# A hybrid trunk on one core: the output projection of the first three tiles moved between the steps of the attention

## The chip, the cores and the metric

The kernel runs on 1 core of a Trainium2 chip. The metric is the device time of one execution in microseconds, the median of three runs.

## What is computed

Two layers, each a pre-norm, one input projection, four branches with a gate each, one output projection, a post-norm and a residual. The sequence has 1024 positions and the model width is 1024; the branches are 256 wide each. The change touches the last two lines of the loop and the attention, cut here to what matters:

```python
def mla_branch(cq, ckv, k_rope, gate, positions, qa_g, qb_w, kva_g, kvb_w):
    q = (rms_norm(cq, qa_g) @ qb_w).reshape(bsz, s, D_HEADS, D_NOPE + D_ROPE)
    ...
    def attend(inp):
        qb, qch = inp
        sc = jnp.einsum('bqhd,bkhd->bhqk', qb, k).astype(jnp.float32) * scale
        mask = key_chunk[None, :] <= qch[:, None]
        p = jax.nn.softmax(jnp.where(mask, sc, MASK_VALUE), axis=-1).astype(v.dtype)
        return jnp.einsum('bhqk,bkhd->bqhd', p, v)
    ...
    return o * jax.nn.silu(gate)

def reference(...):
    for l in range(DEPTH):
        h = rms_norm(x, pre_norm_g[l])
        proj = h @ w_in[l]
        ...
        y = jnp.concatenate([y_a, y_b, y_c, y_d], axis=-1) @ w_out[l]
        x = x + rms_norm(y, post_norm_g[l])
    return x
```

`y_a` is a convolution branch, `y_b` a gated linear recurrence, `y_c` a chunked state-space scan, `y_d` the attention above, causal by blocks. So a query tile late in the sequence has long scores, one early in it has short ones.

## The kernel before

**Tiles.** The sequence is cut into 8 token tiles of 128 rows. From the attention on they are taken from the last to the first: `ORDER` is 7, 6, ..., 0. Products with weights are made in three passes, high part by high part, high by low and low by high (`wh`, `wl` are the two parts of a weight, `yh`, `yl` of the activations).

**Order of work.** Each stage is a Python generator, a "thread"; `weave` takes the next step from the thread whose planned position is lowest (`PLAN` gives start, end and count of steps). A scheduler afterwards orders the instructions of each engine; each engine then works its own list in order. DMAs are issued from SP, POOL and ScalarE.

**Attention**, `th_att`, per tile two half-steps `m` of two heads each: scores `psc` on TensorE (a large PSUM buffer, of which there are two), their maximum `nm` on VectorE (L912), the exponentials `pe` on ScalarE (L914, 7 buffers of the `k4` kind), then transposes `ptp` (L923), copies `pT`, and the product with the values into `poD` (L927). Between them `q_steps` (L861) makes the queries of a later tile: product `pq`, scaling `qk` on ScalarE, rotation on VectorE, transposes `ptq`. At a tile's end the reciprocal of the sums is spread over 256 columns on VectorE (`rsD`, L934), transposed (`prsD`, L937), multiplied with the gate (`gD`) and the result `yD` is stored by POOL into a buffer in memory, `yspF` (L942). Short PSUM tiles come from two small pools of two buffers each, `smA` (`ptp`, `prsD`, `pty` among others) and `smB` (`poD`, `pq`, `ptq`).

**Output projection.** `th_w` loads `w_out` in 8 chunks and splits them. `out_a` (L963) loads one tile of the concatenated branches by two SP transfers, casts and subtracts one half of it (`yh`, `yl`), transposes the other half (`pty`) and does the same. `out_b` (L977) makes the 48 products of a tile (`pz`, L991). `th_o` (L996) does `out_a`, `out_b` of tile 7 and `out_a` of tile 6 at the end of the attention.

**Last phase of a layer.** For each tile `out_b` of it, `out_a` of the one two later, and `out_c` (L1032): load of the residual tile `xt` (2 buffers), Square with its sum on ScalarE into the scratch tile `hn` (2 buffers, L1043), product with the post-norm row `gpost` on VectorE into `zt` (L1044), reciprocal root by two short ScalarE steps (L142, L143), residual (L1049), store; in layer 0 also the next layer's pre-norm: Square (L233), `hn` (L235), 8 transposes `pst` (L239), their split `hh`, `hl`. In layer 1 the result goes out. `th_v` of the next layer (projection rows `psV`) is the first work that uses `hh`, tile by tile.

## Time and profile before

| | us |
|---|---|
| median of three runs | 1264.37 (1259.96 to 1267.64) |
| the profiled execution | 1263.69 |
| its span in the trace | 1261.9 |
| TensorE busy in it | 1197.7 (95%) |
| VectorE busy | 836.2 (66%) |
| ScalarE busy | 478.5 (38%) |
| POOL busy | 183.1 (15%) |

The busy times come from one execution. Matmul ends are modelled in it and overlap the next start, so the busy share of TensorE is not the share in which it does useful work at its full rate; where exact lengths matter they are taken from start to start. Two places matter for what follows: the attention of layer 0 ends at 541 us and that of layer 1 at 1161 us, and the products of layer 0's last phase end at 640 us. A row of a timeline gives in brackets the idle time of its engine ahead of it and what ended that.

### The profile page before, as it was taken

How to read it: one execution, taken by the hardware profiler on the slowest of the kernel's cores; microseconds unless marked ns; L12 is line 12 of the kernel's file. 1: busy time of each engine (PE TensorE's matmuls, PEld its weight loads, DVE VectorE, ACT ScalarE, POOL GpSimd, SP SyncE). 2: the span in 40 equal slices, each digit the busy share in tenths (PEclk: the TensorE clock that was granted, in tenths of full speed). 3: DMA queues.
4: the chain of work that ended last, by engine and by line, in shares of the span. 5: the costliest groups of instructions: out<-in, count | busy, mean ns of one | idle time of the engine just before them, and what ended most of it. 6: DMA issues, size and time to landing. Idle time of an engine off the chain costs nothing.

```text
span 1261.9 us, 17853 instructions
## 1 busy us (share of the span) xinstructions
PE 1197.7 (95%) x6902; PEld 987.0 (78%) x6902; DVE 836.2 (66%) x1579; ACT 478.5 (38%) x1088; POOL 183.1 (15%) x290
## 2 busy tenths in 40 slices
PE   5999999899989989999999999998999998999997
PEld 5988899888878746678898889897888776566886
DVE  5566999985376386745454859999754763867232
ACT  5413322233474374433432222321435644644211
POOL 2100011201133111210020001211012322112000
PEclk9999999999999989989999999998999899999999
DMA  7001122201151040244221111211114311202531
GB/s 274 34 34 68 44 83 85 76 34 48 62 156 61 22 153 23 66 148 147 101 97 67 34 51 59 92 52 67 35 61 123 106 36 54 93 18 68 188 129 71
DMA packets 38660, 101.47 MB, mean 80 GB/s; under 512 B 5440, under 2 KB 13808, under 8 KB 38576
## 3 DMA queue, kind: packets, MB, share of 16 engines
q1 hardware_dynamic: 22848, 51.42, 11.9%
q0 software_dynamic: 14864, 46.04, 11.1%
q10 hardware_dynamic: 864, 2.88, 0.6%
q8 instruction: 54, 0.88, 0.3%
q14 instruction: 30, 0.25, 0.1%
HBM read 75.37 MB, written 25.20 MB: 80 GB/s over the span
## 4 chain that ended last, share of the span: by engine, by line
PE 76%; DVE 14%; ACT 3%; DMA 3%; issue 2%; POOL 0%; DVEq 0%; POOLq 0%; ACTq 0%
PE pz L991 13%; PE psx L220 4%; PE psx L223 4%; PE psx L226 4%; PE psc L909 3%; DVE ca L481 3%; PE plB L625 2%; PE psA L220 2%; PE psA L223 2%; PE psA L226 2%; PE poD L927 2%; PE ptp L923 2%; PE psgA L347 2%; PE psgA L348 2%; PE psgA L349 2%
## 5 line engine op out<-in xcount | busy, mean ns | idle before, releaser
L481 DVE SCALAR_TENSOR_TENSOR ca<-hpad,col,ca 128x512 f32<-128x512 f32 x240 | 186.3, 782 | 3.9
L176 DVE TENSOR_TENSOR wl<-raw,wh 128x1024 fp32r<-128x1024 f32 (+2 forms) x56 | 66.9, 1195 | 92.0 <-ACT wh L160 91.9
L160 ACT CAST wh<-raw 128x1024 fp32r<-128x1024 f32 (+2 forms) x56 | 57.5, 1027 | 139.8 <-PE psA L223 33.7
L991 PE MATMUL pz<-woh,yh 128*128 128x512 f32 x240 | 78.2, 405 | 0.2 <-ACT yh L160 0.2
L991 PE MATMUL pz<-woh,yl 128*128 128x512 f32 x240 | 75.7, 397 | 0.0
L991 PE MATMUL pz<-wol,yh 128*128 128x512 f32 x240 | 75.7, 397 | 0.0
L209 PE MATMUL psg<-wh,hh 128*128 128x256 f32 x256 | 73.9, 289 | 1.5 <-ACT gt L160 1.4
L909 PE MATMUL psc<-kT,qTt 96*128 96x512 f32 (+4 forms) x192 | 73.2, 505 | 0.9 <-ACT pe L914 0.8
L210 PE MATMUL psg<-wl,hh 128*128 128x256 f32 x256 | 73.2, 286 | 0.0
L211 PE MATMUL psg<-wh,hl 128*128 128x256 f32 x256 | 72.8, 284 | 0.0
L914 ACT ACTIVATE pe<-psc,nm 128x1024 f32<-128x1024 f32 (+7 forms) x64 | 47.2, 739 | 64.3 <-DVE nm L912 63.8
L625 PE MATMUL plB<-qz,krb 128*128 128x128 f32 x448 | 63.0, 288 | 8.5 <-DVE krb L635 8.5
L625 PEld LDWEIGHTS plB<-qz,krb 128*128 128x128 f32 x448 | 58.3, 200 | 10.7 <-issue 5.5
L220 PE MATMUL psx<-hh,wh 128*128 128x512 f32 x192 | 62.3, 403 | 0.0
L719 DVE SCALAR_TENSOR_TENSOR xbc<-xpad,col,xbc 128x512 f32<-128x512 f32 x72 | 51.1, 748 | 16.3 <-ACT xbc L172 15.5
L223 PE MATMUL psx<-hl,wh 128*128 128x512 f32 x192 | 61.7, 401 | 0.0
L226 PE MATMUL psx<-hh,wl 128*128 128x512 f32 x192 | 61.1, 397 | 0.0
L991 PEld LDWEIGHTS pz<-wol,yh 128*128 128x128 f32 x240 | 45.6, 190 | 10.6
L176 DVE TENSOR_TENSOR yl<-yt,yh 128x512 fp32r<-128x512 f32 x16 | 11.0, 690 | 64.7 <-ACT yh L160 64.7
L912 DVE TENSOR_REDUCE nm<-psc 128x1 f32<-128x1024 f32 (+7 forms) x64 | 47.2, 745 | 9.9 <-PE psc L909 9.9
L991 PEld LDWEIGHTS pz<-woh,yl 128*128 128x128 f32 x240 | 45.3, 189 | 10.6 <-issue 0.2
L991 PEld LDWEIGHTS pz<-woh,yh 128*128 128x128 f32 x240 | 44.9, 190 | 9.8 <-ACT yh L160 0.4
(331 smaller groups left out, 3052.3 us busy)
## 6 DMA issues: line engine op xcount, KB each, us to landing
raw<-in_w_dram SPq DMA_DIRECT2D x44, 512.0 KB, 3.4
rawo<-in_wo_dram SPq DMA_DIRECT2D x16, 512.0 KB, 4.1
gsp<-gt POOLq DMA_DIRECT2D x16, 256.0 KB, 2.5
gl<-gsp POOLq DMA_DIRECT2D x8, 512.0 KB, 5.0
gspF<-gtA POOLq DMA_DIRECT2D x16, 256.0 KB, 2.3
ysp<-gl POOLq DMA_DIRECT2D x8, 512.0 KB, 3.4
lm<-acsp POOLq DMA_DIRECT2D x16, 256.0 KB, 4.0
yt<-ysp SPq DMA_DIRECT2D x16, 256.0 KB, 3.4
```

What stands on the lines that cost most here:

```text
L160: (V.tensor_copy if name in ONV else A.copy)(out_, in_)
L176: V.tensor_tensor(lo, src, hi.bitcast(F32), op=ALU.subtract)
L209: T.matmul(ps[:, :n], a, hs[k], start=(k == 0), stop=False)
L210: T.matmul(ps[:, :n], a, ls[k], start=False, stop=False)
L211: T.matmul(ps[:, :n], b, hs[k], start=False, stop=(k == KD - 1))
L220: T.matmul(ps[:, h * 512:(h + 1) * 512], w, hh[:, k, h * 512:(h + 1) * 512], start=(k == 0), stop=False)
L223: T.matmul(ps[:, h * 512:(h + 1) * 512], w, hl[:, k, h * 512:(h + 1) * 512], start=False, stop=False)
L226: T.matmul(ps[:, h * 512:(h + 1) * 512], wl, hh[:, k, h * 512:(h + 1) * 512], start=False, stop=(k == KD - 1))
L481: V.scalar_tensor_tensor(t, hp[:, k:k + 512], w[k], t, op0=ALU.mult, op1=ALU.add)
L625: T.matmul(pl[:, o0:o0 + P].rearrange("p (r b u) -> p r b u", r=2, u=u), k_[:, t_ * P:(t_ + 1) * P], z[:, :, t_ * P:(t_ + 1) * P].rearrang ...
L909: T.matmul(psc[:, c0:c1_], qTt[0:k_, h, :], kT[h, c0 // 512][0:k_, 0:c1_ - c0], start=True, stop=True)
L991: T.matmul(pz[n], a[:, k, :], w[:, k, n * 512:(n + 1) * 512], start=(k == 0 and a is yh and w is wh), stop=(k == KD - 1 and a is yl))
```

## The change

Attention and output projection are woven into each other. `th_o` is no longer a thread of the plan but is stepped from `th_att`: at the end of the second tile its first step (a load of `gpost` by POOL and `out_a` of tile 7), then one quarter, 12 products of 512 columns (`pzh`, in a small `smB` bank), after the scores of each half-step of the tiles from the third on. Two quarters make half the columns of an output tile, four a tile, so 12 quarters make the tiles 7, 6 and 5. After each half `post` makes its Square sum and its product with `gpost`; the products are kept in `zt` tiles that take buffers of the weight pools `raw` (twice) and `wh`. Then `out_b` of tile 4 and `out_a` of tile 3 follow. The last phase makes the remaining tiles, and behind the `out_c` of each of the first three of them also the `out_c` of one of the kept tiles. The transposes `prsD` lie in the second half of the bank of `poD`, and the reciprocal is taken on 4 columns, with a copy that spreads it. `w_out` is planned earlier (`w0`, `w1`). The first projection of layer 1 takes the tiles in the order `RORDER`, the order in which the last phase finishes them.

```diff
@@ -23,6 +23,8 @@
+OUT0, NOUT = 2, 3
...
...
+RORDER = [ORDER[n] for n in (3, 0, 4, 1, 5, 2, 6, 7)]
...
-    "o0": (482.2, 511, 8.2),
...
-    "w0": (452.3, 481.6, 8),
+    "w0": (374, 398, 8),
...
@@ -79,9 +82,8 @@
     "c1": (275.5, 340.6, 48.2),
     "d1": (266.1, 351.4, 72),
     "q1": (335.5, 349.5, 2),
-    "o1": (479.4, 508.2, 8.2),
     "att1": (347.1, 481.6, 144.8),
-    "w1": (452.7, 453.2, 8),
+    "w1": (352, 385, 8),
 }
 
 
...
@@ -385,7 +387,7 @@
             hs, ls = load_chunk(l, "v")
             nc.gpsimd.dma_start(out=row, in_=rows[l].partition_broadcast(P))
             nc.gpsimd.dma_start(out=col, in_=cols[l])
-            for n_, i in enumerate(ORDER if l > 0 else range(NT)):
+            for n_, i in enumerate(RORDER if l > 0 else range(NT)):
                 if l == 0:
                     load_x(i + 3)
                     if i > 0:
...
@@ -820,7 +822,7 @@
                 proj_tok(hT, hs, ls, i, ND, ps)
                 ms = small(2, "msd", 3)
                 cn = tmp(384, "cn")
-                jd = br.tile([P, 384], BF16, tag="jd", name="jd", bufs=1)
+                jd = br.tile([P, 384], BF16, tag="jd", name="jd", bufs=1, padded_shape=[P, 512])
                 copy("cn", cn, ps[:, 0:384])
                 krd = small(32, "krd", 2, (P, 2, 16))
                 copy("krd", krd.rearrange("p a j -> p (a j)"), ps[:, 384:416])
...
@@ -890,11 +892,13 @@
             yield next(q_steps)
 
         def th_att():
-            for i in ORDER:
+            outs = th_o()
+            for n_, i in enumerate(ORDER):
                 qTt = qTs[i]
                 n = (i + 1) * P
 
-                po = sm("poD")[:, 0:256]
+                pob = sm("poD")
+                po, prs = pob[:, 0:256], pob[:, 256:512]
                 sume = small(4, "sume", 2)
                 gt = tmp(256, "gD", (P, 2, P))
                 nc.gpsimd.dma_start(out=gt, in_=feat(gspF, 1, i * P, (i + 1) * P))
...
@@ -914,6 +918,8 @@
                         A.activation(pe[:, 0:n], psc[:, 0:n], AF.Exp, bias=nm, accum_out=sume[:, h:h + 1])
                         pes.append(pe)
                     yield i + 1
+                    if n_ >= OUT0:
+                        next(outs, None)
                     for j0 in range(0, i + 1, 4):
                         j1 = min(i + 1, j0 + 4)
                         pts = []
...
@@ -931,8 +937,8 @@
                         next(q_steps, None)
                     yield i + 1
                 rs = tmp(256, "rsD", (P, 4, 64))
-                V.reciprocal(rs, sume.unsqueeze(2).to_broadcast([P, 4, 64]))
-                prs = sm("prsD")[:, 0:256]
+                V.reciprocal(sume, sume)
+                V.tensor_copy(rs, sume.unsqueeze(2).to_broadcast([P, 4, 64]))
                 for m in range(2):
                     T.transpose(prs[:, m * P:(m + 1) * P], rs[:, 2 * m:2 * m + 2, :].rearrange("p h d -> p (h d)"), idn)
                 gf = gt.rearrange("p m t -> p (m t)")
...
@@ -940,7 +946,10 @@
                 y = tmp(256, "yD")
                 V.tensor_tensor(y, po, gf, op=ALU.mult)
                 nc.gpsimd.dma_start(out=feat(yspF, 1, i * P, (i + 1) * P), in_=y.rearrange("p (m t) -> p m t", m=2))
+                if n_ == OUT0 - 1:
+                    next(outs)
                 yield 0.1
+            yield from outs
 
 
         wo_t = {}
...
@@ -993,11 +1002,40 @@
                     yield 1
             zs[i] = pz if halves else [pzb]
 
+        def post(pz, gpost, hv, zt, hn, ss):
+
+            A.activation(hn, pz, AF.Square, scale=1.0 / 32, accum_out=ss)
+            V.tensor_tensor(zt[:, hv], pz, gpost[:, hv], op=ALU.mult)
+
         def th_o():
+
+            gpost = k4("gpost")
+            nc.gpsimd.dma_start(out=gpost, in_=post_g[l].partition_broadcast(P))
             out_a(ORDER[0], lambda: k4("yt"))
             yield 0.1
-            yield from out_b(ORDER[0])
-            out_a(ORDER[1], lambda: k4("yt"))
+            wh, wl = wo_t["h"], wo_t["l"]
+            for n_, i in enumerate(ORDER[:NOUT]):
+                yh, yl = ys[i]
+                zt = wst.tile([P, D], F32, tag=("raw", "raw", "wh")[n_], padded_shape=[P, 1040], name="zt",
+                              bufs=(NRAW, NRAW, NWH)[n_])
+                ss = lay.tile([P, 2], F32, tag="sso", name="sso", bufs=NOUT)
+                for h in range(2):
+                    hv = slice(h * 512, (h + 1) * 512)
+                    pz = sm("pzh")
+                    for k in range(KD):
+                        for a, w in ((yh, wh), (yh, wl), (yl, wh)):
+                            T.matmul(pz, a[:, k, :], w[:, k, hv], start=(k == 0 and a is yh and w is wh),
+                                     stop=(k == KD - 1 and a is yl))
+                        if k == 3:
+                            yield 1
+                    jd = br.tile([P, 512], BF16, tag="jd", name="jz", bufs=1)
+                    post(pz, gpost, hv, zt, jd, ss[:, h:h + 1])
+                    if h == 1:
+                        out_a(ORDER[n_ + 1], lambda: k4("yt"))
+                    yield 1
+                zs[i] = zt, ss
+            yield from out_b(ORDER[NOUT])
+            out_a(ORDER[NOUT + 1], lambda: k4("yt"))
             yield 0.1
 
         def plan(name):
...
@@ -1015,7 +1053,7 @@
         wpool = tc.alloc_tile_pool(name=f"wo{l}", bufs=1, side=my)
         wo_t["h"] = wpool.tile([P, KD, D], F32R, name=f"woh{l}")
         wo_t["l"] = wpool.tile([P, KD, D], F32R, name=f"wol{l}")
-        ths += [Thread(th_att(), *plan("att")), Thread(th_w(), *plan("w")), Thread(th_o(), *plan("o"))]
+        ths += [Thread(th_att(), *plan("att")), Thread(th_w(), *plan("w"))]
         weave(ths, 1e9)
         br.release()
         if l + 1 < L:
...
@@ -1030,18 +1068,20 @@
             gpre = op.tile([P, D], F32, tag="gpre", name="gpre")
             nc.gpsimd.dma_start(out=gpre, in_=pre_g[l + 1].partition_broadcast(P))
         def out_c(i):
-            pz = zs[i]
             tsl = slice(i * P, (i + 1) * P)
             xt = op.tile([P, D], F32, tag="xt", name="xt", bufs=2)
             nc.gpsimd.dma_start(out=xt, in_=(x if l == 0 else xsp)[tsl, :])
-            zt = op.tile([P, D], F32, tag="zt", name="zt", bufs=1)
             hn = op.tile([P, D], F32, tag="hn", name="hn", bufs=2)
-            ss = op.tile([P, 2], F32, tag="ss", name="ssz", bufs=4)
-            nh = len(pz)
-            hv = [slice(h * (D // nh), (h + 1) * (D // nh)) for h in range(nh)]
-            for h, c in enumerate(hv):
-                A.activation(hn[:, c], pz[h], AF.Square, scale=1.0 / 32, accum_out=ss[:, h:h + 1])
-                V.tensor_tensor(zt[:, c], pz[h], gpost[:, c], op=ALU.mult)
+            if isinstance(zs[i], tuple):
+                zt, ss = zs[i]
+                nh, hv = 2, [slice(0, D)]
+            else:
+                zt = op.tile([P, D], F32, tag="zt", name="zt", bufs=1)
+                ss = op.tile([P, 2], F32, tag="ss", name="ssz", bufs=4)
+                nh = len(zs[i])
+                hv = [slice(h * (D // nh), (h + 1) * (D // nh)) for h in range(nh)]
+                for h, c in enumerate(hv):
+                    post(zs[i][h], gpost, c, zt, hn[:, c], ss[:, h:h + 1])
             if nh == 2:
                 V.tensor_tensor(ss[:, 0:1], ss[:, 0:1], ss[:, 1:2], op=ALU.add)
             rstd(ss[:, 0:1], ss[:, 0:1])
...
@@ -1053,13 +1093,16 @@
                 nc.gpsimd.dma_start(out=xsp[tsl, :], in_=xt)
                 pre_norm(hn, xt, gpre, hTn, i)
 
-        for n, i in enumerate(ORDER):
-            if n > 0:
-                for _ in out_b(i):
+
+        for m in range(NOUT, NT):
+            if m + 1 < NT:
+                for _ in out_b(ORDER[m + 1]):
                     pass
-            if n + 2 < NT:
-                out_a(ORDER[n + 2], lambda: op.tile([P, D], F32, tag="yt", name="yt", bufs=2))
-            out_c(i)
+            if m + 2 < NT:
+                out_a(ORDER[m + 2], lambda: op.tile([P, D], F32, tag="yt", name="yt", bufs=2))
+            out_c(ORDER[m])
+            if m - NOUT < NOUT:
+                out_c(ORDER[m - NOUT])
         op.release()
         wpool.release()
         hT = hTn
```

TensorE, layer 0, end of the attention. Names: `ptp` transposes of exponentials, `psc` scores, `prsD` transposes of the reciprocal, `poD` product with the values, `pty` transposes of the branch output, `pz` output products. Before:

```order
L923 MATMUL ptp<-idn,pe 128x128
L909 MATMUL psc<-kT,qTt 128x128
L923 MATMUL ptp<-idn,pe 128x128
L909 MATMUL psc<-kT,qTt 128x128
L937 MATMUL prsD<-idn,rsD 128x128 x2
L923 MATMUL ptp<-idn,pe 128x128
L927 MATMUL poD<-pT,vD 64x128 x2
L923 MATMUL ptp<-idn,pe 128x128
L973 MATMUL pty<-idn,yt 128x128 x4
L937 MATMUL prsD<-idn,rsD 128x128 x2
L927 MATMUL poD<-pT,vD 64x128 x2
L973 MATMUL pty<-idn,yt 128x128 x4
```

After (the quarters are `pzh`, and the reciprocal's transposes are written into `poD`):

```order
L1027 MATMUL pzh<-wol_3926,yh 128x512
L929 MATMUL ptp<-idn,pe 128x128
L913 MATMUL psc<-kT,qTt 128x128
L1027 MATMUL pzh<-woh_3925,yl 128x512
L1027 MATMUL pzh<-woh_3925,yh 128x512
L1027 MATMUL pzh<-wol_3926,yh 128x512
L1027 MATMUL pzh<-woh_3925,yl 128x512
L933 MATMUL poD<-pT,vD 64x128 x2
L982 MATMUL pty<-idn,yt 128x128 x4
L929 MATMUL ptp<-idn,pe 128x128 x2
L1000 MATMUL pz<-woh_3925,yh 128x512 x2
L1000 MATMUL pz<-wol_3926,yh 128x512 x2
```

The rows of tile 0's attention stood next to each other; now products of an output tile lie between them.

ScalarE, layer 0, the attention from tile 6 to tile 5. Names: `pe` exponentials, `qk` scaled queries, `qTt` their transposes copied, `pT` copied transposes of exponentials, `yh` the cast branch output. Before:

```order
L914 ACTIVATE pe,sume<-psc,nm 128x896
L914 ACTIVATE pe,sume<-psc,nm 128x768 x3
L166 ACTIVATE qk<-pq,rq 128x384
L914 ACTIVATE pe,sume<-psc,nm 128x768
L160 COPY qTt<-ptq 96x512
L160 COPY pT<-ptp 128x384
```

After:

```order
L918 ACTIVATE pe,sume<-psc,nm 128x896
L918 ACTIVATE pe,sume<-psc,nm 128x768 x3
L162 CAST yh<-yt 128x4x128
L168 ACTIVATE qk<-pq,rq 128x384
L918 ACTIVATE pe,sume<-psc,nm 128x768
L162 COPY qTt<-ptq 96x512
L162 COPY pT<-ptp 128x384
L162 CAST yh<-pty 128x4x128
```

The two casts of tile 7's branch output now stand in the attention, the first of them ahead of `qk`.

ScalarE, at the end of layer 0's last phase. Names: `hh` cast transposes of the pre-norm, `hn<-xt` Square of the pre-norm, `hn<-pz` Square of the post-norm, `ss`, `ssz` reciprocal roots, `wh<-raw` a weight of layer 1. Before:

```order
L160 CAST hh_4898<-pst 128x4x128 x2
L233 ACTIVATE hn,ss<-xt 128x1024
L142 ACTIVATE ss<-ss,eps 128x1
L143 ACTIVATE ss<-ss 128x1
L160 CAST wh<-raw 128x1024
L1043 ACTIVATE hn,ssz<-pz 128x1024
L160 CAST hh_4898<-pst 128x4x128 x2
L142 ACTIVATE ssz<-ssz,eps 128x1
L143 ACTIVATE ssz<-ssz 128x1
L233 ACTIVATE hn,ss<-xt 128x1024
```

After:

```order
L162 CAST hh_5116<-pst 128x4x128 x2
L1007 ACTIVATE hn,ssz<-pz 128x1024
L144 ACTIVATE ssz<-ssz,eps 128x1
L145 ACTIVATE ssz<-ssz 128x1
L162 CAST wh<-raw 128x1024
L235 ACTIVATE hn,ss<-xt 128x1024
L162 CAST hh_5116<-pst 128x4x128 x2
L1007 ACTIVATE hn,ssz<-pz 128x1024
L144 ACTIVATE ss<-ss,eps 128x1
L144 ACTIVATE ssz<-ssz,eps 128x1
L145 ACTIVATE ss<-ss 128x1
L145 ACTIVATE ssz<-ssz 128x1
```

Two finishing steps are in hand at once there: the short steps of both stand in pairs, and the last post-norm Square stands behind the second pair of casts `hh`.

## Rows read from the trace of the kernel before

**Rows 1.** The page, part 4: chain that ended last, share of the span by engine.

```profile
PE 76%; DVE 14%; ACT 3%; DMA 3%; issue 2%; POOL 0%; DVEq 0%; POOLq 0%; ACTq 0%
```

**Rows 2.** The chain, 536 to 570 us; columns: start us, us, what.

```profile
541.18 12.90 PE pz L991 x48
554.08 0.44 PE pty L973 x4
554.52 11.13 PE pz L991 x48
```

**Rows 3.** Groups of TensorE, 526.9 to 540.8 us; columns: busy, mean, idle before, releasers.

```profile
L923 PE MATMUL ptp<-idn,pe 128*128 128x128 f32 x12 | 2.9, 296 | 1.1 <-ACT pe L914 1.1
L909 PE MATMUL psc<-kT,qTt 100*128 100x128 f32 (+1 forms) x12 | 2.5, 309 | 0.0
L927 PE MATMUL poD<-pT,vD 128*64 128x128 f32 x26 | 2.5, 308 | 0.1
L973 PE MATMUL pty<-idn,yt 128*128 128x128 f32 x8 | 1.7, 354 | 0.0
L937 PE MATMUL prsD<-idn,rsD 128*128 128x128 f32 x6 | 1.6, 350 | 1.9 <-DVE rsD L934 1.7 <-ACT qTt L160 0.2
L866 PE MATMUL pq<-qbt,cqT 128*128 128x384 f32 x4 | 1.6, 512 | 0.0
L879 PE MATMUL ptq<-idn,qk 128*96 128x128 f32 x4 | 0.6, 272 | 0.0
```

**Rows 4.** TensorE's timeline, 503 to 512 us; columns: start us, us, what, count.

```profile
506.53 1.09 PE L927 MATMUL poD<-pT,vD 128*64 128x128 f32 x16
507.55 1.56 PE L866 MATMUL pq<-qbt,cqT 128*128 128x384 f32 x4
508.95 1.02 PE L909 MATMUL psc<-kT,qTt 100*128 100x512 f32 x2
```

**Rows 5.** Mean by stretch; columns: us, busy by engine, TensorE clock, DMA, GB/s.

```profile
538.10:544.90 6.80, 6.08 (x20) 4.55 (x21) 3.96 (x8) 1.71 (x4) 1.44 (x2) 0.50 0.12 39
859.00:863.00 4.00, 0.65 (x6) 0.46 (x5) 4.00 (x7) 0.75 (x2) 0.71 (x1) 0.92 0.16 66
862.40:872.60 10.20, 8.08 (x29) 7.09 (x30) 10.20 (x19) 1.45 (x4) 0.00 (x0) 0.50 0.30 104
1151.00:1161.50 10.50, 8.81 (x60) 5.85 (x60) 8.15 (x23) 5.94 (x21) 2.12 (x3) 1.00 0.37 116
```

**Rows 6.** Timeline, layer 0, 497 to 503 us; in brackets idle before and releaser.

```profile
500.49 1.09 PE L927 MATMUL poD<-pT,vD 128*64 128x128 f32 x16 [0.56 <-DVE pT L160]
```

**Rows 7.** Timeline, layer 1, 1086 to 1094 us.

```profile
1092.37 1.77 PE L909 MATMUL psc<-kT,qTt 96*128 96x512 f32 x4 [0.80 <-ACT pe L914]
```

**Rows 8.** Timeline, layer 0, 475 to 485 us.

```profile
477.80 0.73 POOL L942 DMA_DIRECT2D yspF<-yD  x1 [2.21 <-DVE yD L941]
...
483.37 0.58 ACT L166 ACTIVATE qk<-pq,rq 128x384 f32<-128x384 f32 x1 [0.43 <-PE pq L866]
```

**Rows 9.** DMA issues; columns: queue, count, KB each, median us to landing.

```profile
yt<-yspF SPq DMA_DIRECT2D x16, 256.0 KB, 3.9
xt<-in_x_dram POOLq DMA_DIRECT2D x8, 512.0 KB, 4.2
xsp<-xt POOLq DMA_DIRECT2D x8, 512.0 KB, 2.9
...
yspF<-yD POOLq DMA_DIRECT2D x16, 128.0 KB, 2.2
gpost<-in_post_g_dram POOLq DMA_DIRECT2D x2, 512.0 KB, 6.7
```

**Rows 10.** Timeline, from layer 0 to layer 1, 639 to 652 us.

```profile
640.35 1.02 ACT L1043 ACTIVATE hn<-pz 128x1024 f32<-128x1024 f32 x1
...
643.96 1.28 DVE L1049 SCALAR_TENSOR_TENSOR xt<-zt,ssz,xt 128x1024 f32<-128x1024 f32 x1
...
649.18 1.04 PE L239 MATMUL pst<-idn,hn 128*128 128x128 f32 x8
```

## The prediction

> **What bounds the kernel now.** I read the chain of work that ended last, by engine, first [rows 1]: TensorE holds 76% of it, so a change pays only where it takes idle time, work or slow clock from TensorE. The change neither adds nor removes TensorE work (each weight product, transpose and score of before is there once after), so I looked for places where TensorE stands, and those are the end of the attention in each layer. The last phase itself is full: a tile of output products there costs 11.13 us of matmuls plus 0.44 for its four transposes, back to back [rows 2]. Moving those products saves nothing by itself; what it can save is the idle time that they fill elsewhere.
>
> How much idle there is at the end of layer 0's attention: the groups of TensorE between 526.9 and 540.8 us [rows 3] give the counts, but their modelled lengths overlap, so the work is taken from starts of following rows [rows 4]: 16 poD rows in 1.02 us are 0.064 each, four pq rows in 1.40 are 0.35 each, and two psc rows of 512 columns, listed with 1.02, less the same overlap of 0.16, are 0.43 each. A transpose is 0.11 [rows 2]. So 4 pq make 1.4, 30 transposes (ptp, pty, prsD, ptq) 3.3, the scores with together 2048 columns 1.7, 26 poD 1.7: 8.1 us of work in 13.9, and 5.8 us are idle, the largest piece behind the reciprocal (1.7 by the releaser of prsD [rows 3]). Next the mean clock by stretch [rows 5]: from 538.1 to 544.9 TensorE is granted 0.50 of its clock, 1.2 of 2.4 GHz, and the first product tile takes 12.90 us where the next takes 11.13 [rows 2], so 1.8 us more. Inside the attention there is one gap of 0.56 us in layer 0 [rows 6] and one of 0.80 in layer 1 [rows 7]. The end of layer 1 is 10.5 us long [rows 5] with 60 records, the list of layer 0 less six poD, two prsD and four pty, so 7.0 of work and 3.5 idle, at full clock.
>
> **The change part by part.**
>
> Filling the tails. If every gap above is filled by quarters (12 rows of 512 columns each, taken from the 11.13 us of a tile, so 2.8 us each), layer 0 gives back 5.8 + 1.8 + 0.6 = 8.2 and layer 1 gives back 3.5 + 0.8 = 4.3. That is **-12.5** at most, since nothing else is idle. In the order the quarters stand in blocks between the transposes of the last small tiles, so I take all of it and put the losses apart.
>
> The first quarter. It needs the attention's own output of tile 7: the product on VectorE, a store by POOL to memory, and a load by SP back. In before POOL starts the store at 477.80 [rows 8]; in after the reciprocal's transposes share the poD bank and stand behind one more block, which I estimate at 0.75 us, so 478.55. The store lands 2.2 later, the load takes 3.9 [rows 9], with the hand-over about 485.0. In ScalarE's order the cast of that load stands ahead of the scaling of the queries (qk), which began at 483.37 in before [rows 8]. ScalarE works its rows in order, so qk starts about 485.5, 2.1 late; behind it are the query transposes, then the scores of tile 5, and the quarter itself waits for the same cast, so TensorE has nothing. Bounds: 0, if the hand-over is earlier than I think, and 4.9 if the load takes the 6.7 of the longest 512 KB transfer of that part of the program [rows 9]. I take 2.1 in each layer, as the load's own row is the nearest: **+4.2**. [...]
>
> Other waits in the attention. A quarter may start only when a PSUM buffer of the small pool is free, that is when Square and product of the half before are done, one after the other on ScalarE and VectorE. Bounds: 0 (the half before is two attention steps old) and 0.8 for a late row as in [rows 7] at each of six halves, 4.8 a layer. The engines have slack there, so I am near the lower end: 0.7 a layer, **+1.4**.
>
> The boundary of the layers. Before, a product tile in the last phase carries one finishing step (Square, product, residual, pre-norm, transposes); now five product tiles carry eight, and the last three sets of transposes follow each other closely. In before the last step takes 8.8 us, from its Square at 640.35 to its transposes at 649.18, with the residual at 643.96 [rows 10], and the next layer's first projection (the psV rows) fills almost all of it. In after ScalarE and VectorE have two steps in hand at that point, the kept tile ORDER[2] and the last tile: in ScalarE's order the last Square stands behind the casts of the other's transposes, since the scratch tile hn has two buffers. I replayed the chain with the durations of [rows 10] and their neighbours: the last transposes come 13.0 us after the last product, where TensorE has filler for 9.5. So 3.5 idle against some 0.3 before: **+3.2**. Bounds: 0 (the scheduler's order overlaps better than my replay) and 4.2, the whole growth of the chain.
>
> The clock behind that wait. TensorE stood 3.4 of the 4.0 us from 859.0 to 863.0, and then had 0.50 of its clock for 10.2 us [rows 5], which costs 5.1. Bounds 0 (as at this place in before) and 5.1; I take half: **+2.5**.
>
> At nothing: the reciprocal on 4 columns and a copy, instead of 256 columns, makes VectorE shorter by about an us a tile, and TensorE's part of that is in the tails above. The post-norm row is loaded once more per layer (6.7 us [rows 9], started a tile ahead of its use); its cost would be the same as a late first quarter. Loads and splits of w_out keep their place in the order. The next layer's v weights load later, since the kept products hold the raw buffers, but by the order they are wanted three product tiles, some 33 us, later. The padded jd tile costs only memory.
>
> Sum: -12.5 + 4.2 + 1.4 + 3.2 + 2.5 = -1.2, on the profiled execution's 1263.69, which is 0.7 below the median of the runs (1264.37): **1262.5 us**, no change that a measurement can tell. About 0.5%, 6.3 us, is what a measurement of this kernel tells from no change, so faster means under 1258.1 and slower over 1270.7.
>
> **The rivals.**
>
> *Everything fits.* The first quarter waits little and the boundary stays covered. For it: SP's queue is short there, and the filler of the next layer is long. Against it: ScalarE's order with the cast in front of qk, and the two buffers of hn. Time: 1263.7 - 12.5 + 1.4 = 1252.6, up to 1258 if one of the two places costs its price without the clock.
>
> *The doubled finishing steps bound layer 0's last phase (slower).* Each product tile of 11.13 + 0.44 us and its eight transposes, some 12.4 together, now carries two steps, and the residual tile xt has two buffers. A buffer's round is its load (4.2), the residual's multiply-add (1.28), the store (2.9) beside the pre-norm, and some 2.7 of issues on POOL and waiting for the step beside it: 11.1 [rows 9, 10]. It decides from a load of 5.5 us upward. At the 6.7 us that POOL's load of the post-norm row takes, three pairs lose 1.2 each, 3.6, and the clock falls for another 5.1 as in [rows 5]: 1262.5 + 8.7 = 1271.2. Against it: the xt row itself says 4.2, under the same traffic.
>
> *The change doesn't do what it says.* Excluded as far as the order goes: the quarters do stand between the attention's rows. It could still be that all quarters sit behind a wait, and the tails keep their idle time; then the time is 1263.7 plus the boundary's 5.7, 1269.
>
> **How the numbers follow.** Forecast (stalls at the first quarter and at the boundary, within 1258 to 1269): 0.50. Everything fits: 0.35. Doubled steps: 0.10. Quarters that fill nothing: 0.05. Range: from the end of the fitting case, 1252, to 1270, which leaves out most of the doubled case and a little below. Faster: the fitting case and a small part of the forecast's lower side, 0.38. Slower: 0.10. Same: 0.52.
>
> **What the profile after would show.** In the windows over the end of layer 0's attention, TensorE without idle and a clock of 1.0 where 0.50 stood; the chain there through pzh and psc and no longer through the reciprocal. At the first quarter, the cast of yh with a DMA as releaser, and TensorE idle about 2 us in front of ptq; if that idle is missing, the term of 4.2 is wrong. At the boundary, TensorE idle some 3.5 us in front of the last pst, with hn as what is waited for, and a fall of the clock behind it. The prediction is wrong by most if the two waits are absent, or if xt loads stand in the chain of the last phase.

## The result

The changed kernel takes 1271.69 us (median of 13 runs, 1264.44 to 1276.09) where the kernel before takes 1262.59 (13 runs): a ratio of 1.0057, interval 1.0037 to 1.0078. It is slower by about 7 us, where no measurable change was forecast. The profiled execution of after is 1272.85 us with a span of 1271.0, against 1263.69 and 1261.9; TensorE is busy for 1199.5 us, 94% of the span, with the same 6902 instructions; VectorE for 820.2 instead of 836.2, mainly by the shorter reciprocal. The chain that ended last covers only the final 2% of the span in this trace, so the timelines are read instead.

To see where the 9.2 us between the two profiled executions lie, both are cut at the same rows of TensorE. First the kernel before, then after (timeline; columns: start us, us, engine, line, operation, count): the first scores of layer 0, the first conv projection of layer 1, the first scores of layer 1, the last products.

```profile
448.86 1.06 PE L909 MATMUL psc<-kT,qTt 96*128 96x512 f32 x1
...
650.46 0.50 PE L220 MATMUL psA<-hh,wh 128*128 128x512 f32 x1 [0.24 <-ACT hh L160]
...
1071.56 1.06 PE L909 MATMUL psc<-kT,qTt 96*128 96x512 f32 x1
...
1254.36 0.40 PE L991 MATMUL pzB<-woh,yl 128*128 128x512 f32 x1
```

```profile
450.71 1.06 PE L913 MATMUL psc<-kT,qTt 96*128 96x512 f32 x1
...
654.98 0.79 PE L222 MATMUL psA<-hh,wh 128*128 128x512 f32 x1
...
1074.43 1.21 PE L913 MATMUL psc<-kT,qTt 96*128 96x512 f32 x1
...
1263.68 0.40 PE L1000 MATMUL pzB<-woh,yl 128*128 128x512 f32 x1
```

Attention and last phase of layer 0, up to layer 1's conv projection, take 204.3 us instead of 201.6; those of layer 1 take 189.3 instead of 182.8. That is +2.7 and +6.4, and these two stage lengths are used for every kernel below. Ahead of the attention after stands 1.9 later and between the layers it makes up 1.7; TensorE's rows are the same there, the stretches at the lower clock lie elsewhere.

A stage length holds the lower clock of its one execution as well as the idle time. Both executions have the same mean granted clock, 0.982, but in before layer 0's stage has the stretch at 538.1 and the end of another (445.9 to 452.7), up to 5.4 us lost together, and in after 1.4. So the idle time tells more: TensorE's gaps of 0.3 us and more add up to 3.8 us in layer 0's stage before and 9.5 after, and to 4.3 and 7.7 in layer 1's. The growth, 5.7 and 3.4, together 9.1 us, is the whole difference of the two executions; ahead of and between the stages they come out even (2.0 less and 2.1 more).

The clock in four stretches of after (mean by stretch; columns as in [rows 5]): the stretch at 0.50 that cost 1.8 us in before at 538.1 is gone, and three others, each behind a wait of the changed kernel, have come.

```profile
538.10:544.90 6.80, 6.73 (x43) 4.17 (x41) 4.55 (x12) 3.23 (x9) 0.72 (x1) 1.00 0.06 19
654.20:657.60 3.40, 3.40 (x11) 2.63 (x10) 2.44 (x11) 2.16 (x8) 2.16 (x6) 0.50 0.25 67
1115.00:1118.40 3.40, 3.02 (x21) 2.69 (x22) 0.96 (x3) 1.43 (x4) 0.00 (x0) 0.50 0.00 0
1203.80:1207.20 3.40, 3.40 (x15) 2.35 (x13) 1.47 (x4) 0.59 (x1) 0.00 (x0) 0.50 0.00 0
```

### The profile page after: what moved, and what is told of

Its sections match the earlier page's. It is cut to its first block, busy times and chain, and to the rows that moved or that the text cites. A ratio compares the mean times of both kernels' runs of the same rounds, so it can differ in the third digit from the quotient of the medians.

```text
span 1271.0 us, 17879 instructions
## 1 busy us (share of the span) xinstructions
PE 1199.5 (94%) x6902; PEld 987.7 (78%) x6902; DVE 820.2 (65%) x1607; ACT 479.8 (38%) x1100; POOL 184.2 (14%) x292
## 5 line engine op out<-in xcount | busy, mean ns | idle before, releaser
L162 DVE COPY pT<-ptp 128x512 f32<-128x512 f32 (+3 forms) x72 | 39.0, 551 | 44.7 <-PE ptp L929 44.3
L350 PE MATMUL psgA<-hl,wh 128*128 128x512 f32 x128 | 51.0, 398 | 0.0
L929 PE MATMUL ptp<-idn,pe 128*128 128x128 f32 x288 | 46.1, 279 | 5.1 <-ACT pe L918 3.4
L349 PE MATMUL psgA<-hh,wh 128*128 128x512 f32 x128 | 50.7, 396 | 0.0
L913 PEld LDWEIGHTS psc<-kT,qTt 96*128 96x128 f32 (+1 forms) x192 | 33.4, 196 | 22.1 <-issue 18.0
L351 PE MATMUL psgA<-hh,wl 128*128 128x512 f32 x128 | 50.5, 396 | 0.0
L211 PEld LDWEIGHTS psg<-wh,hh 128*128 128x128 f32 x256 | 48.2, 188 | 2.7 <-ACT gt L162 2.4
```

What stands on the lines that cost most here:

```text
L162: (V.tensor_copy if name in ONV else A.copy)(out_, in_)
L211: T.matmul(ps[:, :n], a, hs[k], start=(k == 0), stop=False)
L913: T.matmul(psc[:, c0:c1_], qTt[0:k_, h, :], kT[h, c0 // 512][0:k_, 0:c1_ - c0], start=True, stop=True)
```

## What the trace of after shows, place by place

**The first quarter.** Timeline of layer 0 (the last bracket is the engine's idle time and what ended it):

```profile
486.88 0.62 ACT L162 CAST yh<-yt 128x512 fp32r<-128x512 f32 x1 [1.96 <-DMA yt<-yspF]
487.40 0.57 ACT L168 ACTIVATE qk<-pq,rq 128x384 f32<-128x384 f32 x1
...
489.17 0.61 PE L881 MATMUL ptq<-idn,qk 128*96 128x128 f32 x4 [0.58 <-DVE qk L877]
...
490.54 1.09 PE L933 MATMUL poD<-pT,vD 128*64 128x128 f32 x16 [0.76 <-DVE pT L162]
```

The same rows in layer 1:

```profile
1111.71 0.62 ACT L162 CAST yh<-yt 128x512 fp32r<-128x512 f32 x1 [2.79 <-DMA yt<-yspF]
...
1114.00 0.61 PE L881 MATMUL ptq<-idn,qk 128*96 128x128 f32 x4 [1.41 <-DVE qk L877]
...
1115.38 1.97 PE L933 MATMUL poD<-pT,vD 128*64 128x128 f32 x16 [0.76 <-DVE pT L162]
```

ScalarE stands for its load, 1.96 and 2.79 us, and begins qk behind the cast (layer 0; the order is the same in layer 1), where in before qk waited 0.43 for the product alone [rows 8]. The load takes 3.8 us by its median, 3.9 in [rows 9]. TensorE then stands 0.58 + 0.76 in layer 0 and 1.41 + 0.76 in layer 1, and in layer 1 the stretch at 0.50 from 1115.0 follows at once: the 16 poD rows that take 1.09 in [rows 4] take 1.97.

**The end of the attention**, layer 0:

```profile
573.25 0.60 ACT L1007 ACTIVATE jz<-pzh 128x512 bf16<-128x512 f32 x1
...
573.97 0.69 DVE L1008 TENSOR_TENSOR zt<-pzh,gpost 128x512 f32<-128x512 f32 x1 [0.32 <-ACT jz L1007]
...
575.08 0.30 PE L929 MATMUL ptp<-idn,pe 128*128 128x128 f32 x1 [0.86 <-ACT sso L144]
...
575.20 0.57 ACT L162 CAST yh<-pty 128x512 fp32r<-128x512 f32 x1
...
576.34 0.72 PE L1000 MATMUL pz<-woh,yh 128*128 128x512 f32 x2 [0.96 <-ACT yh L162]
```

The last quarter is over before the attention is. Behind it come the Square of the last kept half (jz), its product (zt) with the post-norm row, and only then, in VectorE's order, the copy of the transposes (574.65 to 574.93); the casts of tile 4 (yh) stand behind the same Square and its reciprocal root (sso, 574.76 to 575.05) in ScalarE's order. TensorE waits 0.86, which the bracket puts down to sso, and 0.96 for yh. Layer 1 has the same two gaps, and then the stretch at 0.50 from 1203.8.

**The boundary of the layers:**

```profile
643.98 1.04 ACT L1007 ACTIVATE hn<-pz 128x1024 f32<-128x1024 f32 x1
...
652.26 1.28 DVE L237 SCALAR_TENSOR_TENSOR hn<-xt,ss,gpre 128x1024 f32<-128x1024 f32 x1
...
653.68 1.46 PE L241 MATMUL pst<-idn,hn 128*128 128x128 f32 x8 [2.92 <-DVE hn L237]
```

The last Square begins at 643.98, 3.3 us after the last product started (0.9 in before), behind the transposes that free its hn and the casts of them; its own transposes start 2.92 us late, 9.7 after it, where before they came 8.8 after it [rows 10]. Without these 2.9 us layer 0's stage would be as long as in before's execution, which had up to 4 us more of lower clock in it.

**A residual tile in layer 1:**

```profile
1233.95 1.28 DVE L1089 SCALAR_TENSOR_TENSOR xt<-zt,sso,xt 128x1024 f32<-128x1024 f32 x1 [4.92 <-DMA xt<-xsp]
...
1236.43 0.73 PE L1000 MATMUL pz<-woh,yh 128*128 128x512 f32 x2 [0.96 <-DVE zt L1008]
```

The multiply-add of a kept tile waits 4.92 us for its xt; the product of the fresh tile (zt) stands behind it on VectorE and holds the PSUM bank that pz waits for, 0.96. The steps come in pairs: the first two multiply-adds of layer 0's last phase start at 594.97 and 596.40, so both xt are being stored at once.

## The experiments

Each ratio is to the kernel before, run on the same chip, with its interval; stage lengths are those of the one profiled execution. A stretch at 0.50 that falls into a stage in one execution and not in another changes its length by up to half of 3.4 or 6.8 us, so a difference of that size is read with the gaps beside it. The earlier loads of w_out and the order `RORDER` were not run by themselves.

**Four single edits of the changed kernel.** Theory A: new waits at the places above; theory B: weaving the rows costs by itself.

The first step of the output thread half a step later:

```diff
-                if n_ == OUT0 - 1:
-                    next(outs)
```

> The changed kernel with one edit: the first step of the output thread (post-norm load, load and casts of tile 7's branch output) is taken in the place of the first quarter, half a step later, so that in ScalarE's order the cast of yh stands behind qk; the last quarter falls behind the attention. Theory A (the added time comes from three new waits: the cast ahead of qk, the last kept half's Square and product ahead of the casts of tile 4 at the attention's end, and the finishing steps at the layers' boundary, each followed by a stretch at 1.2 GHz): the idle of 1.3 us in layer 0 and 2.5 in layer 1 goes, with 1.7 of clock in layer 1, so 5.5 less than the changed kernel, about 1266. Theory B (weaving rows of 512 columns between the attention's rows itself costs, wherever the waits are): no change from 1271.7.

Measured: 1275.63, ratio 1.0090 (1.0067 to 1.0113). Layer 1 is 183.3, 5.9 shorter, the size that theory A had but not its place: the first quarter still waits 1.41 there (at 1122.20), and what is gone are the two gaps at the attention's end, the gap behind xt and two stretches at 0.50, while gaps of 0.35 to 0.98 have come at later tiles. Layer 0 is 212.8, 8.5 longer, most of it in its last phase, where TensorE waits 2.82 for zt at 602.57 and 2.68 for a weight's split (wl) at 633.56, with a stretch at 0.50 behind each. TensorE's wait at the first quarter only changed its place:

```profile
487.16 0.62 ACT L162 CAST yh<-yt 128x512 fp32r<-128x512 f32 x1 [1.21 <-DMA yt<-yspF]
...
487.81 0.69 DVE L178 TENSOR_TENSOR yl<-yt,yh 128x512 fp32r<-128x512 f32 x1 [0.95 <-ACT yh L162]
...
489.29 1.15 DVE L162 COPY pT<-ptp 128x512 f32<-128x512 f32 x2
...
490.02 1.09 PE L933 MATMUL poD<-pT,vD 128*64 128x128 f32 x16 [1.25 <-DVE pT L162]
```

qk is ahead of the cast now, but VectorE's subtraction (yl) waits for the cast, the copies pT stand behind it, and poD waits 1.25.

Tile 4's casts half a tile earlier:

```diff
-                    if h == 1:
+                    if h == (0 if n_ == NOUT - 1 else 1):
                         out_a(ORDER[n_ + 1], lambda: k4("yt"))
```

> The changed kernel with one edit: loads and casts of tile 4 (ORDER[3]) are written half a tile earlier, after the first half of the last kept tile, so that they no longer stand behind the last half's Square, product and reciprocal root. Theory A: the two gaps of 1.02 and 1.15 us at the end of the attention go in both layers, and 1.7 of slow clock in layer 1: 6 less than the changed kernel, about 1266. Theory B: 1271.7.

Measured: 1278.73, ratio 1.0106 (1.0083 to 1.0128); layer 1 is 184.4, 4.8 shorter, layer 0 214.9, 10.6 longer. In layer 0's last phase:

```profile
611.88 0.53 POOL L1073 DMA_DIRECT2D xt<-in_x_dram  x1 [3.49 <-DMA xsp<-xt]
...
615.83 1.28 DVE L1089 SCALAR_TENSOR_TENSOR xt<-zt,sso,xt 128x1024 f32<-128x1024 f32 x1 [5.72 <-DMA xt<-in_x_dram]
617.03 1.22 DVE L1008 TENSOR_TENSOR zt<-pz,gpost 128x1024 f32<-128x1024 f32 x1
...
618.31 1.22 PE L1000 MATMUL pz<-woh,yh 128*128 128x512 f32 x2 [6.41 <-DVE zt L1008]
```

A load of xt is issued only when the store of the earlier step that used its buffer has landed, the multiply-add waits 5.72 us for it, the fresh tile's product with the post-norm row is behind that, and TensorE stands for 6.41 us. This is the second rival of the prediction, in a kernel that only had tile 4's casts half a tile earlier.

Three hn instead of two (`name="hn", bufs=3`):

> The changed kernel with one edit: three scratch tiles hn in the last phase instead of two. Theory A: the last Square of layer 0 no longer waits for the transposes of the kept tile; of the 2.9 us of idle in front of the last transposes 2 go, with the 1.7 of slow clock behind them: about 1268. Theory B: 1271.7. A third reading, that the chain of ScalarE and VectorE is too long whatever the buffers: also 1271.7, with the 2.9 us still in the trace.

Measured: 1268.31, ratio 1.0028 (1.0007 to 1.0049). Layer 0 is 199.7, 4.6 shorter, without the gap and without the stretch at 0.50; the boundary's wait and its price are as theory A has them. The intervals of this kernel and of after overlap; the trace shows the gap gone.

All quarters behind the attention (`OUT0, NOUT = 8, 3`):

> The changed kernel with one edit: all twelve quarters behind the attention (products still kept on chip, finishing steps still doubled, w_out and the reciprocal as changed). Theory A: the ends of the attention idle as in the kernel before (8.2 and 4.3 us less some 1.5 for the shorter reciprocal), the boundary costs its 5, the waits at the first quarter and the attention's end are gone: 1262.6 + 5 - 1.5, about 1266. Theory B: the rows are not woven, the same 1266 or less; what tells here is the trace: whether the ends of the attention in this kernel idle more or less than the 1.3 to 2.5 and 2.2 us of the woven one.

Measured: 1275.07, ratio 1.0090 (1.0065 to 1.0116), a miss for both theories: layer 1 185.0, layer 0 211.7. Nothing is woven here, and layer 0 still loses 10 against before. Its last phase:

```profile
598.11 0.70 PE L1000 MATMUL pz<-woh,yh 128*128 128x512 f32 x2 [2.37 <-DVE zt L1008]
...
613.41 0.73 PE L1000 MATMUL pz<-woh,yh 128*128 128x512 f32 x2 [1.30 <-DVE zt L1008]
...
626.01 1.29 DVE L1089 SCALAR_TENSOR_TENSOR xt<-zt,sso,xt 128x1024 f32<-128x1024 f32 x1 [5.06 <-DMA xt<-in_x_dram]
...
628.51 0.39 PE L212 MATMUL psV<-wl,hh 128*128 128x260 f32 x1 [2.16 <-DVE wl L178]
```

With 2.96 in front of the boundary's transposes, TensorE waits 8.8 us here, each time behind VectorE's list of finishing steps, one of which stands 5.06 us for its xt. So the doubled steps cost without any weave. The changed kernel has the same steps behind its product tiles and waits in layer 0 almost only at the boundary; why they fall better there isn't shown. At the ends of the attention, which the expectation asked for, the gaps add up to 2.7 and 3.1 us here and to 1.8 in either layer of the woven kernel.

**Three xt, and the edits together.**

```diff
-            xt = op.tile([P, D], F32, tag="xt", name="xt", bufs=2)
+            xt = op.tile([P, D], F32, tag="xt", name="xt", bufs=3)
```

> The changed kernel with one edit: three residual tiles xt in the last phase instead of two. Theory A2 (the two earlier edits lost their gain because a finishing step's xt load must wait for the store of the step two before it; with doubled steps that chain of store, load and multiply-add on VectorE holds the PSUM bank of the product tile): the gap of 1.1 us at 1235 us in layer 1 goes, layer 0's stays as it is (it waits for hn): about 1270.5. Theory C (the finishing steps are slow by VectorE's work, not by xt): 1271.7 with the same gap.

Measured: 1265.97, ratio 1.0018 (1.0002 to 1.0034), by the ratios 5 less than after, more than expected: layer 1 is 188.1, without the gap at xt, and layer 0 201.7, so the boundary's gap went with it too. I had put that gap on hn alone; either buffer removes it.

> The changed kernel with four edits together: the output thread's first step half a step later, tile 4's casts half a tile earlier, three xt, and the post-norm Square written to a scratch tile of its own, so that the two hn serve the pre-norm alone. Theory A2: the gaps of 6.4, 2.8 and 2.8 us that the first two edits alone had in layer 0's last phase are gone, and what they gained in layer 1 (5.9 and 4.8) stays: layer 0 from its first scores to layer 1's first conv projection 196 (before 201.6, the changed kernel 204.3), layer 1 from its first scores to the end 182 (182.8, 189.3), the time about 1256. Theory B (weaving itself costs) or C: 1264 or more.

Edit: the first two edits, three xt, and a scratch tile for the Square:

```diff
+            jz2 = op.tile([P, D], BF16, tag="jz2", name="jz2", bufs=1)
...
-                    post(zs[i][h], gpost, c, zt, hn[:, c], ss[:, h:h + 1])
+                    post(zs[i][h], gpost, c, zt, jz2[:, c], ss[:, h:h + 1])
```

Measured: 1274.67, ratio 1.0089 (1.0063 to 1.0114), a miss: 206.0 and 187.8. The large gaps of the last phase are gone, but the first quarter's wait now comes back at later tiles, since casts and subtractions of a branch output stand ahead of qk again:

```profile
552.83 0.61 ACT L162 CAST yh<-yt 128x512 fp32r<-128x512 f32 x1
...
554.79 0.69 DVE L178 TENSOR_TENSOR yl<-pty,yh 128x512 fp32r<-128x512 f32 x1
...
555.47 0.58 ACT L168 ACTIVATE qk<-pq,rq 128x384 f32<-128x384 f32 x1 [0.20 <-PE pq L868]
...
557.91 0.61 PE L881 MATMUL ptq<-idn,qk 128*96 128x128 f32 x4 [0.98 <-DVE qk L877]
```

> The kernel with the four edits, and besides the finishing step of a kept tile written ahead of the products of the next tile instead of behind the step of the fresh one (and layer 1's first projection in that order). Theory A2: the steps no longer come in pairs behind one product tile, the boundary has one step in hand; some 1 to 3 less than the kernel with four edits, about 1254. Theory C: no change against it.

Measured: 1274.07, ratio 1.0077 (1.0052 to 1.0102); 209.5 and 188.9. No gain from the other sequence of the steps.

**The start one tile later**, on the kernel with three xt (`OUT0, NOUT = 3, 3`):

> The changed kernel with three xt, and the output thread started one tile later (OUT0 = 3): its load and casts at the end of the third tile, ten quarters in the attention, two behind it. In the order of ScalarE the cast of yh now stands behind qk, the scores' exponentials and the copies. Theory A2: the wait at the first quarter (1.65 + 0.92 us in layer 1, 1.7 in layer 0 of the kernel with three xt) goes, and nothing takes its place: 4 less than the kernel with three xt, about 1262. Theory D (a transfer that a cast waits for stalls whichever row stands behind it; moving the start moves the stall): no change from 1266.

Measured: 1267.52, ratio 1.0031 (1.0015 to 1.0048). Layer 1 is 182.4, 5.6 shorter than with three xt alone. The first quarter's gaps there (1.48, 0.76 and 1.30) are gone, and at the attention's end 1.3 stand instead of 1.8, so the 5.6 are not the first quarter alone. Layer 0 is 207.4, with the boundary's gap back.

> The changed kernel with three xt, and tile 4's load and casts half a tile earlier. Theory A2: with xt free the gain of that edit is no longer given back in the last phase; 1.02 + 1.15 us in each layer and 1.7 of clock go: 5 less than the kernel with three xt, about 1261. Theory D: the casts wait for their transfer ahead of the last kept half's rows, so the time stays at 1266 or rises.

Measured: 1276.47, ratio 1.0099 (1.0077 to 1.0121): the early casts alone lose on this kernel too (212.8 and 186.4), now with 3.66 us in front of transposes at 614.48, behind the split hl on VectorE.

> Both of these edits on the kernel with three xt. Theory A2: the gains add, about 1258, under the kernel before. Theory D: 1266 or more.

Measured: 1266.61, ratio 1.0023 (1.0006 to 1.0040); 206.3 and 182.6. Again layer 0 gives back at the boundary what layer 1 gained:

```profile
645.22 1.04 ACT L1007 ACTIVATE hn<-pz 128x1024 f32<-128x1024 f32 x1
...
650.50 1.94 PE L241 MATMUL pst<-idn,hn 128*128 128x128 f32 x8 [2.96 <-DVE hn L237]
```

> The kernel with three xt and the later start, with two kept tiles instead of three (eight quarters, all inside the attention, two doubled finishing steps). Theory A2: the doubled steps cost nothing any more with three xt, and tile 5 fills the end of the attention as whole product tile: about 1262, as with three tiles. Theory B (each woven quarter costs, 144 rows of 0.242 us against 0.232 in the last phase): a third less of that, 1 less than with three tiles.

Edit: `OUT0, NOUT = 3, 2` on the kernel with three xt, and the order (2, 0, 3, 1, 4, 5, 6, 7). Measured: 1276.66, ratio 1.0107 (1.0078 to 1.0136), a miss on both theories: layer 0 is 205.8, layer 1 191.1. The last phase opens with the post-norm row, three xt and two yt under way at once, and TensorE waits 4.02 us for the second yt.

**The largest waits taken away**: three xt, the start one tile later, a scratch tile for the Square; then also tile 4's casts early.

> The changed kernel with three xt, the start one tile later, and the post-norm Square written to a scratch tile of its own instead of hn. Theory A2: the 2.9 us in front of the transposes at the boundary and the half of a 6.8 us stretch at 1.2 GHz behind it go: layer 0 from its first scores to layer 1's conv projection 201 instead of 207.4 (before 201.6), the time about 1261. Theory B (weaving itself costs): 1266.

Measured: 1262.47, ratio 0.9985 (0.9966 to 1.0004), 202.7 and 182.9. Against the same kernel without the scratch tile (1.0031) that is 6 us less by the ratios and 4.7 in layer 0, up to 3 of them lower clock.

> The same with tile 4's casts half a tile earlier. Theory A2: 206.3 of layer 0 becomes 200, layer 1 stays at 182.5: about 1260. Theory B: 1265.

Measured: 1259.21, ratio 0.9976 (0.9959 to 0.9994), 202.6 and 181.9. The boundary in this kernel:

```profile
638.29 1.03 ACT L1007 ACTIVATE jz<-pz 128x1024 bf16<-128x1024 f32 x1
...
648.60 1.17 PE L241 MATMUL pst<-idn,hn 128*128 128x128 f32 x8 [1.53 <-DVE hn L237]
```

Counted from the start of layer 0's last product (638.55 and 636.75), the last Square begins 6.7 us after it in the kernel without the scratch tile and 1.5 after it in this one, and the wait is 1.53 instead of 2.96. One more large wait is left in layer 0, behind a late yt, and in layer 1 three that the quarters bring themselves (layer 0 has the same three):

```profile
597.78 0.70 PE L1000 MATMUL pz<-woh,yh 128*128 128x512 f32 x2 [1.68 <-DVE zt L1008]
...
1138.44 0.77 PE L933 MATMUL poD<-pT,vD 128*64 128x128 f32 x10 [0.68 <-DVE pT L162]
...
1177.36 0.50 PE L1027 MATMUL pzh<-woh,yh 128*128 128x512 f32 x1 [0.46 <-DVE zt L1008]
...
1186.03 0.44 PE L933 MATMUL poD<-pT,vD 128*64 128x128 f32 x4 [0.53 <-DVE pT L162]
```

With nearly the same weave (started one tile later, with two of the twelve quarters behind the attention), then, a time 10 us below the changed kernel by the ratios: theory B falls as an account of the loss. It doesn't follow that the weave gains. The gaps of 0.3 us and more in the two stages add up to 13.3 us here and to 8.1 in before; what is lower is the loss by the clock, whose mean over the runs is 0.9865 against 0.9840 for before on the same chip, some 3 us, as much as the kernel gains. And the reciprocal alone, below, gives the same ratio. Why the clock is higher isn't shown.

From the kernel with four edits this one differs only in where the output thread starts (its quarters one half-step later, the load and casts of tile 7 somewhat more), and by 14 us; why the casts fall so much better here I can tell for single rows, not for the whole.

**The reciprocal by itself.** The kernel before with one part of the change:

```diff
-                V.reciprocal(rs, sume.unsqueeze(2).to_broadcast([P, 4, 64]))
+                V.reciprocal(sume, sume)
+                V.tensor_copy(rs, sume.unsqueeze(2).to_broadcast([P, 4, 64]))
```

> The kernel before with one part of the change: the reciprocal on 4 columns and a copy to 256, instead of 256 columns. It takes 1.2 us from VectorE in each tile, of which the end of layer 0 waits 1.7 and the gap in layer 1 0.8: about 2 less than before, and 1.8 more if the slow clock at 538 us goes too, so 1259 to 1261. If the ends wait for something else right behind, 1262.6.

Measured: 1260.74, ratio 0.9977 (0.9958 to 0.9996), so 2.9 us less; the stages are 199.9 and 180.8, 1.7 and 2.0 less. The groups of TensorE and the clock at the end of layer 0, which answer to [rows 3] and [rows 5]:

```profile
L938 PE MATMUL prsD<-idn,rsD 128*128 128x128 f32 x6 | 1.3, 291 | 0.2 <-ACT qTt L160 0.2
```

```profile
538.10:544.90 6.80, 6.04 (x33) 4.84 (x34) 3.18 (x7) 2.12 (x4) 1.45 (x2) 1.00 0.12 39
```

The 1.9 us ahead of prsD are 0.2, and in this execution the clock stays at 1.00.

> The changed kernel with the reciprocal over 256 columns as before. If the shorter reciprocal gives in the woven kernel what it gave alone (2.9), about 1274.5, and the weave alone costs some 10; if quarters hide the reciprocal, 1271.7.

Measured: 1270.37, ratio 1.0068 (1.0043 to 1.0092), no different from after. The long reciprocal (1.75 us) is there at the end of the attention and one gap grows from 0.86 to 1.63, but the other is shorter:

```profile
570.56 1.75 DVE L940 RECIPROCAL rsD<-sume 128x256 f32<-128x256 f32 x1 [0.53 <-ACT pe L918]
...
573.27 0.30 PE L929 MATMUL ptp<-idn,pe 128*128 128x128 f32 x1 [1.63 <-ACT sso L144]
```

## Why the prediction was wrong, step by step

**Filling the tails, -12.5: the step that failed.** I took the whole idle time as given back because quarters stand between the last tiles' rows. But the quarters end at 573.1 us, before the last tile's attention does, and the work that follows them, Square, product, casts of tile 4, is a new end with 1.8 us of idle in each layer and a stretch at 0.50 behind it in layer 1 (1.7).

The size was wrong as well. I worked out 5.8 and 3.5 us of idle at the two ends from counts of rows at full clock, although 2.7 us of layer 0's window lie in the stretch at 0.50 [rows 5], where rows take longer without any idle time. The idle that the trace records there is 1.1 + 0.1 + 1.9 = 3.1 us in layer 0 [rows 3] and 1.6 in layer 1, most of it ahead of this row (groups of TensorE in before, 1151.0 to 1161.5 us):

```profile
L923 PE MATMUL ptp<-idn,pe 128*128 128x128 f32 x12 | 2.9, 296 | 1.3 <-ACT pe L914 1.2
```

With the 1.8 of clock and the gaps of 0.6 and 0.8 that leaves 5.5 (up to 1.3 more by the slow rows inside the window) and 2.4 to be had instead of 8.2 and 4.3.

Nor did the weave come free. In the kernel without the largest waits layer 1 is 0.9 shorter than before and layer 0 is 1.0 longer. Against the 2.4 of layer 1 stand 1.7 for the three gaps of the quarters and 1.1 for the woven rows themselves, which take 0.242 us from start to start (144 rows in 34.8 us in either layer) where layer 1's product rows of before take 0.234. Against the 5.5 of layer 0 stand the same 1.7 and 1.1, 0.8 in front of scores at 492.59, and 3.2 (1.5 at the boundary, 1.7 for a product tile whose bank is held behind a late yt). Those sums give 0.4 longer and 1.3 longer; since the stretches at the lower clock fall differently in the two executions, a fit within some 1.5 us is as much as can be said. What the weave fills it takes back in its own waits and rows.

**The reciprocal at nothing: not contradicted where it was put, but a cheaper change was missed.** In the woven kernel the long reciprocal costs nothing that the runs can tell (1.0068 against 1.0057), so it was right to put its 1.7 us in the tails and not to count them twice. Alone it gives 2.9 us, as much as the whole weave with its largest waits removed (0.9977 and 0.9976). I did not see that this small part gets as much without the rest.

**The first quarter, +2.1 a layer: right in place, short in price.** Counted from the first scores of layer 0, qk begins 2.2 us later than before, 2.1 forecast. The idle is 1.3 and 2.2 us, but in layer 1 the lower clock behind it costs another 1.7. I priced that only for the boundary.

**The boundary, +3.2: right.** From the last product (640.71) to the conv projection (654.98) it takes 14.3 us against 11.0 before, 3.2 more, and the last transposes start 13.0 after the last product, as in the replay. The clock behind it, +2.5: 3.4 us at 0.50, so 1.7.

**Other waits, +0.7 a layer: about right.** A quarter waits 0.37 us in layer 0 (at 513.99) and 0.61 in layer 1 (at 1140.48), but for the copy qTt, not for Square and product of the half before as I had it.

**The rival of the doubled steps: right as a mechanism, wrong in its deciding point.** I made it depend on a load of 5.5 us, with one use of each buffer per product tile, evenly spaced; the loads take 4.6 and the stores 3.3 by their medians in after, which would still fit by that round (4.6 + 1.28 + 3.3 + 2.7 = 11.9 of 12.4). But the two steps of a pair come together, both buffers are stored at once, each load is issued only when its buffer's store has landed, and VectorE's order then puts the fresh tile's product behind the wait. In after it costs 1 us in layer 1 and a part of layer 0's boundary; three xt alone take 5 off by the ratios. That this rival's 1271.2 lies next to the measured 1271.69 is chance: it had its loss in three pairs of layer 0, where after waits almost only at the boundary.

By these terms layer 1 was forecast at -1.5 and came out at +6.4: 2.2 and 1.7 at the first quarter, 1.8 and 1.7 at the end, 1.0 for xt, 1.1 for the woven rows, 9.5 together, which leaves about 3 as gained. Layer 0 was forecast at +0.3 and came out at +2.7; there the gaps grew by 5.7, and up to 4.0 us less of lower clock fell into the stage.

## What to carry to other kernels

Take the idle time to be filled from the gaps that the trace records, and not from a count of rows at their best rate. Then look at what the filler itself leaves behind on the in-order engines when it ends: here it made a new end of 1.8 us a layer. When a stage's finishing steps are doubled up, follow each of their buffers through store, reload and use before counting on them, and give the reloaded tile a third buffer first. Before moving work into a gap, ask what makes the gap: here an operation on fewer columns gave as much as the weave did at its best.

## What the runs showed of the hardware

A wait of one to three microseconds on TensorE is paid twice when a stretch at 1.2 GHz follows: 3.4, 6.8 or 10.2 us long in these traces, up to half of it lost. In after 1.41 + 0.76 us of idle in layer 1 are followed by one, 0.58 + 0.76 at the same place in layer 0 are not; 0.85 + 0.96 at the end of the attention are in layer 1 and 0.86 + 0.96 are not in layer 0. How much of a run is at the lower clock differs between runs of the same kernel, and that is most of the spread: the 13 runs of after go from 1264.44 us at a mean granted clock of 0.988 to 1276.09 at 0.978.

Transfers that start together took far longer than usual. In the kernel with two kept tiles a load of yt is issued at 1202.65, while the post-norm row and three xt are under way, and its cast begins at 1213.92 (10.9 us to landing by the median of the two such loads there); the same load takes 3.8 us by its median in after.

```profile
1202.65 1.28 SPq L976 DMA_DIRECT2D yt<-yspF  x1
...
1213.92 0.62 ACT L162 CAST yh<-yt 128x512 fp32r<-128x512 f32 x1 [10.60 <-DMA yt<-yspF]
```
